# Six PSUM banks in one pool, products of heads and of a layer's last group issued elsewhere, and a first load in halves: a two-layer trunk on one core

## The chip, the core and the metric

The kernel runs on one core of a Trainium2 chip. The metric is the device time of one execution in microseconds, from runs on the chip. Five engines of the core work at the same time, each through its own instructions in order: TensorE (PE, with its weight loads apart as PEld), VectorE (DVE), ScalarE (ACT), GpSimd (POOL) and SyncE (SP, which here only issues transfers). PE writes its results to PSUM, eight banks of 128 partitions x 512 fp32 values; DVE and ACT read them from there into SBUF.

## The reference

Two layers over x of 512 tokens x 1024 features in fp32 (batch 1). Cut to what is computed:

```python
for i in range(2):
    xn = rmsnorm(x, norm1_g[i])
    u_pool, q, k, v, g_a, g_b = split(xn @ w_in[i])       # 1024 wide each
    # 4 heads, two q/k maps of 128 each, v of 256
    q = rotary(rmsnorm(q, q_norm_g[i])); k = rotary(rmsnorm(k, k_norm_g[i]))
    p = softmax(mask(q @ k.T * 128 ** -0.5))              # chunk-causal, chunks of 64
    o = (p[map 0] - lam * p[map 1]) @ v
    o = rmsnorm(o, subln_g[i]) * (1 - lam_init)
    pool = concat over 4 groups of (mean of the last 2/4/8/16 tokens of u - u) @ w_pool
    merged = sigmoid(g_a) * pool * pool_scale + sigmoid(g_b) * o
    x = x + merged @ w_out[i]
    gate, up = split(rmsnorm(x, norm2_g[i]) @ w_ffn_in[i])   # 2816 wide each
    x = x + (silu(gate) * up) @ w_ffn_out[i]
```

## The kernel before

**Products.** Every fp32 operand is split into a high part `...h`/`hi` (a cast on ACT) and a remainder `...l`/`lo` (a subtraction on DVE), in `split` (L208; the function's rows have L210). A product of two operands is three matmuls: high x high, high x low, low x high (`product`, L294; `in_turn`/`three`, L277 to L292). A product of 128 tokens x 512 columns over the 1024 features is 24 matmuls. Weights come in pieces of 512 KB in the order of `weight_plan`, into seven `raw` buffers, and are split into `whi`/`wlo` (six buffers). Almost all of a layer's DVE work beside the splits is reading results from PSUM.

**Order.** A scheduler of the framework sets the order on each engine from the order in which the code issues the work; buffers and banks are handed out in turn by pool name, and an instruction that takes a buffer waits for its last reader. Work that has to wait for a transfer or another engine is put off by hand: `later(delay, f)` puts `f` on a heap with a due time in PE columns, and `run_due` runs what is due between two products. PSUM has four pools: `mm` (three banks), `sc` (two), `tr` (two), and one bank `oy`, whose two halves take the attention outputs in turn (`o_ps`) and which as a whole takes every second out-unit of the feed-forward part (`unit_bank`).

**A layer, first half.** The four heads in the order 3, 2, 1, 0 (`ORDER`). `attention(j)` makes q and k of the head in four token tiles `t`; `evicted` reads each bank (squares on ACT, `r` on POOL at L344, `qn` on DVE at L597), rotates, and transposes by way of a transfer to HBM and back (`turned`). Then follow, by due times, `turn` (splits into `qh`, `ql`), `scores(t)` (bank `sc`, softmax into `pr`), `turn_prob` (splits into `ah`, `al`) and `weighted(t)` (the product with v; `mt` at L565 reads the result). Between two heads `mix(i)` calls `merged`: the pooled inputs u (`up`, `us`, then `uh`, `ul`), the two gate products (`ta`, L686), the pool's product with `pw`, and the merged result of the head as `mh`/`ml` (L214, L215). `project_out` (L762) multiplies the merged result of the first or second head with its rows of w_out and adds it to the residual `res`; `attention` calls it through `then` in the third and fourth head, after tile 0. `last_out` (L771) does the same for the last two heads together, eight outputs with 12 matmuls each: six of head 1, six of head 0.

**Second half.** `odd_group`, then five groups of four hidden blocks. Each group makes its gate and up products with seven instead of eight smaller products (`PRODUCTS`, in the order 1, 4, 5, 6, 2, 7, 3), from sums of inputs and weights; pairs of banks are `a` (`sc`), `b` (`mm`) and `c` (`tr`). Product 5 writes `c`, DVE reads it into `cah`/`cal` (L928) after product 7, and product 3 writes `c` anew. `UNITS` says after which product of which group an out-unit stands (24 matmuls with the hidden values of an earlier group). Last come the out-units of the last two groups.

**The start.** Twelve bf16 matmuls on zeros run first. `first_step(i)` loads two feature blocks of weights (`wr`) and of x (`xr`), 512 KB each; for i = 0 the split and the scaling by the gain (`xh`, `xl`) are already done in halves.

## Time and profile before

| | before |
|---|---|
| median of 3 runs | 1393.08 us (1391.87 to 1394.55) |
| the profiled execution | 1394.02 us, its span 1392.2 us |
| granted TensorE clock | 1.00 |
| PE busy | 1375.2 us (99%), 6242 matmuls |
| DVE busy | 1045.5 us (75%), 1979 instructions |
| ACT busy | 703.3 us (51%) |
| POOL busy | 117.7 us (8%) |
| HBM traffic | 160 GB/s over the span |

The rows of the trace name an engine, the line of the kernel, the output tile `<-` the input tiles, a shape and a count. In brackets stands the idle time of the engine just before, and what ended it. The table of waits adds these idle times by line and releaser: total, times, longest. In the chain of waits each piece starts where the one before released it.

### The profile page before, as it was taken

To read this page: it belongs to the slowest core of one execution; us is meant where nothing else is said; L and a number is where in the kernel's file an instruction comes from. 1 tells how busy PE (TensorE), PEld (TensorE's weight loads), DVE (VectorE), ACT (ScalarE), POOL (GpSimd) and SP (SyncE) were. 2 spreads that over 40 slices of the span, in tenths; PEclk is the share of its full clock that TensorE was granted. 3 is DMA by queue.
4 is the path that set the end of the run, shared out by engine and by line. 5 is a ranking of instruction groups with operands and counts; after the bars stand their busy time and mean duration, and the time that the engine had idled before them with its cause. 6 is when DMAs were issued, how large, how long until landed. Compare 5 with 4: busy or idle time off the path is not lost.

```text
span 1392.2 us, 18593 instructions
## 1 busy us (share of the span) xinstructions
PE 1375.2 (99%) x6242; PEld 1138.3 (82%) x6242; DVE 1045.5 (75%) x1979; ACT 703.3 (51%) x1321; POOL 117.7 (8%) x139
## 2 busy tenths in 40 slices
PE   9999999999999999999999999999999999999998
PEld 7888788887888888887887787888878888888877
DVE  7769788686968768677668896877868687676782
ACT  7445353454756545554345543434447565565540
POOL 1010100000101001000010101000001010000000
PEclk9999999999999999999999999999999999999999
DMA  7333454445667868676434445544446788677741
GB/s 300 113 124 112 143 164 128 146 130 146 133 178 197 224 190 230 161 199 195 134 102 138 124 142 179 161 133 126 150 137 136 188 211 212 195 207 179 183 137 61
DMA packets 140783, 224.52 MB, mean 161 GB/s; under 512 B 40848, under 2 KB 88464, under 8 KB 140688
## 3 DMA queue, kind: packets, MB, share of 16 engines
q1 hardware_dynamic: 130176, 187.65, 42.0%
q0 software_dynamic: 9216, 33.56, 13.9%
q10 hardware_dynamic: 1296, 2.12, 0.5%
q8 instruction: 49, 0.80, 0.2%
q14 instruction: 46, 0.38, 0.1%
HBM read 194.04 MB, written 29.23 MB: 160 GB/s over the span
## 4 chain that ended last, share of the span: by engine, by line
PE 89%; DVE 6%; issue 1%; POOL 1%; DMA 1%; ACT 1%; SPq 0%; DVEq 0%; POOLq 0%; ACTq 0%
PE mm L299 11%; PE mm L300 11%; PE mm L301 11%; PE mm L281 8%; PE mm L282 8%; PE mm L280 8%; PE tr L280 3%; PE tr L281 3%; PE tr L282 3%; PE oy L281 3%; PE oy L280 3%; PE oy L282 3%; PE sc L280 3%; PE sc L281 3%; PE sc L282 3%
## 5 line engine op out<-in xcount | busy, mean ns | idle before, releaser
L210 ACT CAST whi<-raw 128x1024 fp32r<-128x1024 f32 (+1 forms) x221 | 230.2, 1047 | 175.7 <-PE mm L300 42.0
L210 DVE TENSOR_TENSOR wlo<-raw,whi 128x1024 fp32r<-128x1024 f32 (+1 forms) x221 | 267.0, 1212 | 63.1 <-ACT whi L210 62.2
L299 PE MATMUL mm<-whi,xh 128*128 128x512 f32 x480 | 188.9, 394 | 1.0 <-DVE qn L597 1.0
L301 PE MATMUL mm<-whi,xl 128*128 128x512 f32 x480 | 187.3, 390 | 0.0
L300 PE MATMUL mm<-wlo,xh 128*128 128x512 f32 x480 | 187.3, 390 | 0.0
L301 PEld LDWEIGHTS mm<-whi,xl 128*128 128x128 f32 x480 | 90.2, 188 | 19.0
L299 PEld LDWEIGHTS mm<-whi,xh 128*128 128x128 f32 x480 | 90.3, 188 | 18.6 <-PE mm L301 1.4
L300 PEld LDWEIGHTS mm<-wlo,xh 128*128 128x128 f32 x480 | 90.3, 188 | 17.3
L236 POOL DMA_DIRECT2D wlo<-in_wts x64 | 56.1, 877 | 552.3 <-ACT wlo L235 423.0
L344 POOL TENSOR_TENSOR r<-r,mhalf 128x1 f32<-128x1 f32 (+1 forms) x64 | 56.7, 887 | 525.0 <-DVE r L343 422.0
L300 PE MATMUL mm<-xl,whi 128*128 128x512 f32 x256 | 99.9, 390 | 0.0
L299 PE MATMUL mm<-xh,whi 128*128 128x512 f32 x256 | 99.9, 390 | 0.0
L301 PE MATMUL mm<-xh,wlo 128*128 128x512 f32 x256 | 99.7, 390 | 0.0
L703 DVE TENSOR_TENSOR res<-mm,res 128x512 f32<-128x512 f32 x96 | 65.3, 682 | 32.3 <-PE mm L282 27.5
L235 ACT ACTIVATE wlo<-raw 128x1024 fp32r<-128x1024 f32 x64 | 67.7, 1057 | 26.8 <-PE mm L281 25.2
L234 ACT CAST whi<-raw 128x1024 fp32r<-128x1024 f32 x64 | 66.6, 1040 | 18.3 <-issue 17.7
L280 PE MATMUL oy<-fh,whi 128*128 128x512 f32 (+1 forms) x180 | 69.7, 387 | 0.0
L281 PE MATMUL oy<-fl,whi 128*128 128x512 f32 (+1 forms) x180 | 69.7, 387 | 0.0
L282 PE MATMUL oy<-fh,wlo 128*128 128x512 f32 (+1 forms) x180 | 69.7, 387 | 0.0
L280 PE MATMUL mm<-fh,whi 128*128 128x512 f32 (+1 forms) x176 | 68.1, 387 | 0.0
L282 PE MATMUL mm<-fh,wlo 128*128 128x512 f32 (+1 forms) x176 | 68.1, 387 | 0.0
L281 PE MATMUL mm<-fl,whi 128*128 128x512 f32 (+1 forms) x176 | 68.1, 387 | 0.0
(244 smaller groups left out, 3231.4 us busy)
## 6 DMA issues: line engine op xcount, KB each, us to landing
raw<-in_wts SPq DMA_DIRECT2D x244, 512.0 KB, 4.1
wlo<-in_wts POOLq DMA_DIRECT2D x64, 512.0 KB, 6.2
away<-near SPq DMA_DIRECT2D x72, 256.0 KB, 2.3
near<-away SPq DMA_DIRECT2D x288, 64.0 KB, 2.2
away<-near SPq DMA_DIRECT2D x28, 128.0 KB, 1.7
near<-away SPq DMA_DIRECT2D x112, 32.0 KB, 2.4
res<-in_x_t SPq DMA_DIRECT2D x4, 512.0 KB, 7.7
pwr<-in_pool_w ACTq DMA_DIRECT2D x8, 256.0 KB, 2.6
```

Of the source, the lines that this page charges most:

```text
L210: return nc.scalar.copy(hi, src), nc.vector.tensor_sub(lo, src, hi.bitcast(F32))
L234: nc.scalar.copy(hi, raw)
L235: made[0] = nc.scalar.activation(lo, raw, AF.Copy, scale=-1.0)
L236: nc.gpsimd.dma_start(lo.rearrange("p a b -> p (a b)"), wts[piece_no], accum_op=ALU.add)
L280: nc.tensor.matmul(acc, lhsT=ah, rhs=bh, start=start, stop=False, **check)
L281: nc.tensor.matmul(acc, lhsT=ah, rhs=bl, start=False, stop=False, **check)
L282: last = nc.tensor.matmul(acc, lhsT=al, rhs=bh, start=False, stop=stop, **check)
L299: nc.tensor.matmul(acc, lhsT=ah, rhs=bh, start=i == 0, stop=False)
L300: nc.tensor.matmul(acc, lhsT=ah, rhs=bl, start=False, stop=False)
L301: last = nc.tensor.matmul(acc, lhsT=al, rhs=bh, start=False, stop=i == n - 1)
L344: nc.gpsimd.tensor_tensor(r, r, mhalf[:, :width], op=ALU.pow)
L703: return nc.vector.tensor_add(res[d][:, cs], acc, res[d][:, cs])
```

## The change

It has five parts. The pools `tr` and `oy` are gone and `mm` has six banks; transposes, attention outputs and out-units draw from it. `project_out` is called after tile 1. `last_out` issues, for its first pair of outputs, the products of head 1 into both banks and then those of head 0. The out-unit (2, 3) of the last group stands after product 7 instead of after product 4; the weight plan follows. The first weights and the first x are loaded in two transfers each, in turn.

```diff
-         (3, 7): [(2, 0)], (3, 3): [(2, 1)], (4, 1): [(2, 2)], (4, 4): [(2, 3)]}
+         (3, 7): [(2, 0)], (3, 3): [(2, 1)], (4, 1): [(2, 2)], (4, 7): [(2, 3)]}
...
     def mm_ps():
-        return ps.tile([P, 512], F32, name="mm", tag="mm", bufs=3)
+        return ps.tile([P, 512], F32, name="mm", tag="mm", bufs=6)
...
-    def tr_ps():
-        return ps.tile([P, 512], F32, name="tr", tag="tr", bufs=2)
-
-    oy = ps.tile([P, 2, VD], F32, name="oy", tag="oy")
-    turns = [0]
-
-    def o_ps():
-        turns[0] += 1
-        return oy[:, turns[0] % 2, :]
+    tr_ps = mm_ps
...
-    def in_turn(acc, pairs, start=True):
+    def in_turn(acc, pairs, start=True, stop=True):
...
-                last = three(acc, a, b, start and not i, i == len(pairs) - 1)
+                last = three(acc, a, b, start and not i, stop and i == len(pairs) - 1)
...
-        nc.sync.dma_start(wr, wts[i].rearrange("p (a s) -> p a s", a=2))
-        nc.sync.dma_start(xr, x_t[i].rearrange("p (a s) -> p a s", a=2))
+        for ks in (slice(0, 1), slice(1, 2)) if not i else (slice(0, 2),):
+            for to, src in ((wr, wts), (xr, x_t)):
+                nc.sync.dma_start(to[:, ks, :], src[i].rearrange("p (a s) -> p a s", a=2)[:, ks, :])
...
-                o = s_ps()[:, :VD] if at_start and t % 2 else o_ps()
+                o = mm_ps()[:, :VD]
...
-                if not t and then is not None:
+                if t == 1 and then is not None:
                     then()
...
-        def unit_bank(n):
-            return oy.rearrange("p a b -> p (a b)") if n % 2 else mm_ps()
...
         def last_out(x):
             for i in range(4):
                 w = piece(4)
+                accs = [mm_ps() for _ in range(2)]
+                pairs = [[(cols(w, a)[2 * n + h], (ms[j][0][:, h, :], ms[j][1][:, h, :]))
+                          for n, j in enumerate(ORDER[2:]) for h in range(2)] for a in range(2)]
+                if not i:
+                    for a in range(2):
+                        in_turn(accs[a], pairs[a][:2], stop=False)
                 for a in range(2):
-                    acc = mm_ps()
-                    in_turn(acc, [(cols(w, a)[2 * n + h], (ms[j][0][:, h, :], ms[j][1][:, h, :]))
-                                  for n, j in enumerate(ORDER[2:]) for h in range(2)])
-                    x.added = add_out(i + 4 * a, acc)
+                    in_turn(accs[a], pairs[a][0 if i else 2:], i > 0)
+                    x.added = add_out(i + 4 * a, accs[a])
                 x.put(i)
...
-                units[0] += 1
-                acc = unit_bank(units[0])
+                acc = mm_ps()
```

The numbers of matmuls and of the other instructions stay as they are, but for the two more transfers on SP. The lines of the changed kernel are eight to ten lower for the same code (L299 becomes L290).

In the last group of layer 1 PE goes from product 7 (`xr` operands, the `mm` bank) straight to product 3 (`xh`, the `tr` bank of `cah`):

```order
L280 MATMUL mm_12340<-whi_12422,xrh_10125 128x512
L281 MATMUL mm_12340<-wlo_12423,xrh_10125 128x512
L282 MATMUL mm_12340<-whi_12422,xrl_10126 128x512
L280 MATMUL tr_12121<-whi_12485,xh_9886 128x512
L281 MATMUL tr_12121<-wlo_12486,xh_9886 128x512
L282 MATMUL tr_12121<-whi_12485,xl_9887 128x512
L280 MATMUL tr_12121<-whi_12485,xh_9886 128x512
L281 MATMUL tr_12121<-wlo_12486,xh_9886 128x512
```

In the changed kernel the unit's 24 matmuls (`fh`, `fl`, two banks of 12) stand between them:

```order
L271 MATMUL mm_12377<-whi_12459,xrh_10180 128x512
L272 MATMUL mm_12377<-wlo_12460,xrh_10180 128x512
L273 MATMUL mm_12377<-whi_12459,xrl_10181 128x512
L271 MATMUL mm_12527<-fh_11196,whi_12523 128x512
L272 MATMUL mm_12527<-fl_11197,whi_12523 128x512
...
L272 MATMUL mm_12541<-fl_11199,whi_12523 128x512
L273 MATMUL mm_12541<-fh_11198,wlo_12524 128x512
L271 MATMUL mm_12190<-whi_12566,xh_9941 128x512
L272 MATMUL mm_12190<-wlo_12567,xh_9941 128x512
L273 MATMUL mm_12190<-whi_12566,xl_9942 128x512
```

What moved is the unit, from behind product 4 of the same group to the place between the two.

In layer 1, second head, PE issues the weighted product of tile 2 (`ah`, `al`, into `oy`) behind both gate products (`mm_7854` is the second) and the first matmul with `pw`:

```order
L299 MATMUL mm_7854<-xh_6352,whi_7615 128x512
L300 MATMUL mm_7854<-xl_6353,whi_7615 128x512
L301 MATMUL mm_7854<-xh_6352,wlo_7616 128x512
L299 MATMUL mm_7883<-uh_7624,pw_7621 128x512
L299 MATMUL oy_66<-vh_7356,ah_7731 128x256
L300 MATMUL oy_66<-vl_7357,ah_7731 128x256
L300 MATMUL mm_7883<-ul_7625,pw_7621 128x512
L301 MATMUL mm_7883<-uh_7624,pw_7621 128x512
L299 MATMUL mm_7922<-uh_7624,pw_7621 128x512
L301 MATMUL oy_66<-vh_7356,al_7732 128x256
L299 MATMUL oy_66<-vh_7356,ah_7731 128x256
```

In the changed kernel it stands (into `mm_7862`) behind the first gate product, `mm_7841`, and ahead of the second, `mm_7900`:

```order
L290 MATMUL mm_7841<-xh_6388,whi_7658 128x512
L291 MATMUL mm_7841<-xl_6389,whi_7658 128x512
L292 MATMUL mm_7841<-xh_6388,wlo_7659 128x512
L290 MATMUL mm_7862<-vh_7399,ah_7775 128x256
L291 MATMUL mm_7862<-vl_7400,ah_7775 128x256
L292 MATMUL mm_7862<-vh_7399,al_7776 128x256
...
L291 MATMUL mm_7862<-vl_7400,ah_7775 128x256
L292 MATMUL mm_7862<-vh_7399,al_7776 128x256
L290 MATMUL mm_7900<-xh_6388,whi_7640 128x512
L291 MATMUL mm_7900<-xl_6389,whi_7640 128x512
```

It moved up by the 24 matmuls of a gate product and one of the pool's. On DVE the split that makes its `al` stood here, behind the sums `us` of the pooled inputs and one weight split:

```order
L686 TENSOR_TENSOR ta_7851<-mm_7796,hg_6484 128x512
L661 MEMSET us_7787 128x16
L662 TENSOR_TENSOR us_7787<-us_7784 128x512
L210 TENSOR_TENSOR wlo_7952<-raw_7949,whi_7951 128x1024
L665 TENSOR_TENSOR head_7790<-us_7787,tab_69 128x16
L666 SCALAR_TENSOR_TENSOR us_7787<-us_7787,up_7775 128x496
L210 TENSOR_TENSOR al_7732<-pr_7526,ah_7731 128x384
L668 TENSOR_TENSOR us_7787<-head_7790,up_7775 128x16
L686 TENSOR_TENSOR ta_7880<-mm_7854,hg_6484 128x512
```

In the changed kernel it stands behind the same sums, without that weight split, and ahead of the evacuation `ta` of the second gate as before:

```order
L678 TENSOR_TENSOR ta_7897<-mm_7841,hg_6523 128x512
L653 MEMSET us_7832 128x16
L654 TENSOR_TENSOR us_7832<-us_7829 128x512
L648 MEMSET up_8666 128x16
L657 TENSOR_TENSOR head_7835<-us_7832,tab_68 128x16
L658 SCALAR_TENSOR_TENSOR us_7832<-us_7832,up_7820 128x496
L660 TENSOR_TENSOR us_7832<-head_7835,up_7820 128x16
L653 MEMSET us_8669 128x16
L201 TENSOR_TENSOR al_7776<-pr_7569,ah_7775 128x384
```

On DVE it moved by one weight split only.

## The prediction

> **What bounds the kernel now.** I read the page's busy times first, then the waits of TensorE, then the rows around each wait.

> ```profile
> span 1392.2 us, 18593 instructions
> PE 1375.2 (99%) x6242; PEld 1138.3 (82%) x6242; DVE 1045.5 (75%) x1979; ACT 703.3 (51%) x1321; POOL 117.7 (8%) x139
> ```

> TensorE is the bound: 6242 matmuls fill 99% of the span. The change keeps every matmul, so it can only win idle time of PE. All of that idle time stands in one short table (total, times, longest):

> ```profile
> PE mm L299 <- DVE qn L597: 3.5, 2, 2.4
> PE tr L280 <- DVE cah L928: 3.1, 2, 1.6
> PE oy L299 <- DVE mt L565: 1.7, 3, 0.8
> PE mm L391 <- DVE us L661: 1.2, 1, 1.2
> PE mm L280 <- ACT mh L214: 1.2, 2, 0.6
> PE tr L462 <- DVE xh L454: 0.8, 1, 0.8
> PE mm L299 <- ACT mh L214: 0.6, 1, 0.6
> PE mm L281 <- DVE ml L215: 0.5, 2, 0.2
> PE sc L300 <- DVE ql L210: 0.4, 1, 0.4
> PE sc L301 <- DVE al L210: 0.3, 1, 0.3
> PE mm L300 <- DVE ml L215: 0.2, 1, 0.2
> ```

> The L391 row is the wait of the warm-up matmuls for a memset and stays, as does the `al` row (first head of layer 0). The rest sums to 12.0 us. The table counts from the modelled end of the matmul before, so it is short. These rows (start, duration) give the correction:

> ```profile
> 646.06 0.39 PE L280 MATMUL mm<-whi,xrh 128*128 128x512 f32 x1
> 646.29 0.39 PE L281 MATMUL mm<-wlo,xrh 128*128 128x512 f32 x1
> 646.51 0.39 PE L282 MATMUL mm<-whi,xrl 128*128 128x512 f32 x1
> 648.47 0.47 PE L280 MATMUL tr<-whi,xh 128*128 128x512 f32 x1 [1.57 <-DVE cah L928]
> ```

> A matmul lasts 0.39 us but the next starts 0.227 us after it, so each wait costs some 0.16 us more than the table says: here 648.47 - 646.51 - 0.227 = 1.73, against 1.57. With 0.16 for each of these 15 waits, some 14 us are there to win: a perfect change ends near 1380, 1% below the 1394.0 us of the profiled execution (span 1392.2 and 1.8 around it). That execution is 0.9 above the median 1393.08; I sum against 1394.0 and take 0.9 off at the end. A difference under 0.2% (2.8 us) is about what a measurement cannot tell from none.

> **The change part by part.**

> *Halves at the start.* The chain of waits at the start, and the DMA rows for sizes:

> ```profile
> 0.74 4.61 DMA raw<-in_wts
> 5.38 0.63 ACT whi L210
> 6.03 0.60 DVE wlo L210
> 6.67 0.50 DVE xh L454
> 7.31 0.47 PE tr L462
> 1.19 5.30 PE L391 MATMUL mm<-cold 128*128 128x512 bf16 x12 [1.19 <-DVE us L661]
> raw<-in_wts SPq DMA_DIRECT2D x244, 512.0 KB, 4.1
> pwr<-in_pool_w ACTq DMA_DIRECT2D x8, 256.0 KB, 2.6
> ```

> The cast, the subtraction and the scaling already work on halves; only the two transfers (weights, x) are whole. 256 KB land in 2.6 us elsewhere, 512 KB in 4.1: 1.5 less. The chain behind it keeps its length, and the warm-up matmuls end at 1.19 + 5.30 = 6.49 by the record (the last of them could be followed at about 6.3), so at most 1.0 can be won. At worst nothing is: the two more issues on SP push the later transfers back. I take 0.8, near the cap, because 1.5 is well over it.

> [...]

> *`project_out` after the second token tile.* It was called after tile 0 and consumed `mh`/`ml` of an earlier head too early. In layer 0:

> ```profile
> 146.45 0.40 PE L301 MATMUL mm<-mh,wlo 128*128 128x512 f32 x1
> ...
> 148.50 0.39 PE L301 MATMUL mm<-mh,wlo 128*128 128x512 f32 x1
> ```

> Three steps take 2.05 instead of 0.68: 1.37 lost. One more tile is 24 matmuls, 24 x 0.227 = 5.4 us, in front of it: gone (between 1.37 and 0, and the cover is four times the need).

> *`last_out`, both layers.* The two head-2 products of both accumulators now come first, 12 matmuls instead of 6 ahead of the first use of the last head.

> ```profile
> 340.83 0.39 PE L280 MATMUL mm<-mh,whi 128*128 128x512 f32 x1
> ...
> 343.62 0.39 PE L282 MATMUL mm<-mh,wlo 128*128 128x512 f32 x1
> ```

> Five steps took 2.79 instead of 1.13: 1.66. The cover is 6 x 0.227 = 1.36; I take 1.3 in each layer, 2.6 (bounds 0 and 3.3). The first `put` comes 1.4 later for it; it feeds the odd group, behind three more rounds of 12 matmuls.

> *The unit after product 7.* In the last group of each layer product 3 waits for `cah` (1.73 above, about the same in layer 1). Now 24 matmuls, 5.4 us, stand between: both go, 3.4. Product 5 loses the unit that stood ahead of it. Groups 0 and 1 have none there either, and no wait of such a product is in the table: nothing.

> *Six banks, heads of layer 1.* Gone: the longer of the two waits for `qn`, 2.4 + 0.16 = 2.6 (a `project_out` whose bank `qn` still reads), and the other, 1.1 + 0.16 = 1.2 (a bank too); the three of `oy` behind `mt`, 1.7 + 3 x 0.16 = 2.2, since the weighted products no longer share one bank; the 0.6 at `ql`. That is 6.6.

> But the same pool lets the order issue the weighted products of the first two heads earlier, ahead of where their operands are ready. The second head, before (DVE rows, PE row, then windows with busy time of PE, PEld, DVE, ACT, POOL):

> ```profile
> 806.19 0.69 DVE L657 TENSOR_TENSOR up<-mm,hg 128x512 f32<-128x512 f32 x1 [2.05 <-PE mm L301]
> ...
> 823.21 1.22 DVE L210 TENSOR_TENSOR wlo<-raw,whi 128x1024 fp32r<-128x1024 f32 x1
> ...
> 825.02 0.56 DVE L210 TENSOR_TENSOR al<-pr,ah 128x384 fp32r<-128x384 f32 x1
> 825.01 0.39 PE L299 MATMUL oy<-vh,ah 128*128 128x256 f32 x1
> 826.05 0.28 PE L301 MATMUL oy<-vh,al 128*128 128x256 f32 x1
> 810.00:815.00 5.00, 5.00 (x25) 4.18 (x24) 4.95 (x15) 0.20 (x1) 0.54 (x1) 1.00 0.38 120
> 815.00:820.00 5.00, 5.00 (x26) 4.22 (x25) 4.51 (x15) 2.12 (x7) 0.98 (x1) 1.00 0.50 169
> 820.00:825.00 5.00, 5.00 (x23) 3.95 (x21) 5.00 (x12) 4.03 (x6) 0.00 (x0) 1.00 0.66 216
> ```

> The product of tile 2 uses `al` 0.5 us after DVE wrote it. The order now puts it one gate product ahead: 24 matmuls and one of the pool's, 25 x 0.227 = 5.7 us earlier, so PE asks for `al` at about 819.7 on this clock (its first matmul, 825.01 - 5.7 = 819.3, and two more). On DVE only the 1.22 of `wlo` goes from in front of `al`. From `up` at 806.19, where DVE last waited for PE, `al` ended after 825.58 - 806.19 = 19.4 us; less 1.22, and less the 0.54 us that DVE is idle in the three windows, 17.6. PE needs it after 819.7 - 806.2 = 13.5. New wait: 4.1, with ends 0 (DVE less behind than counted) and 6.3 (`al` as late as before). Behind this product in PE's queue stand the second gate's, and then everything: nothing hides it.

> The first head, tile 3:

> ```profile
> 773.50 1.22 DVE L210 TENSOR_TENSOR wlo<-raw,whi 128x1024 fp32r<-128x1024 f32 x1
> ...
> 775.35 0.48 DVE L565 SCALAR_TENSOR_TENSOR mt<-oy,r,hg 128x256 f32<-128x256 f32 x1 [0.43 <-POOL r L344]
> 775.75 0.68 DVE L210 TENSOR_TENSOR al<-pr,ah 128x512 fp32r<-128x512 f32 x1
> 776.51 0.35 PE L301 MATMUL oy<-vh,al 128*128 128x256 f32 x1
> ```

> `al` comes behind two `wlo`, and now ahead of that `mt`: it would end 1.1 to 1.8 earlier, about 775. PE asks 2.2 (the `oy` waits gone) and about 2.0 (its new place) earlier, near 772.3. New wait between 0 and 776.43 - 772.3 = 4.1; I take 3.0. The scores of tile 2 of the next head stand 1.3 us earlier on PE, behind the same `ql` split that cost 0.6: 0 to 2.1, taken as 1.7. Together +8.8 against -6.6: the front of layer 1 costs 2.2 us net, with ends -6.6 (no new wait) and +5.9.

> *The other banks.* A bank of the pool now comes round after six uses instead of three, and nearly all uses are of 24 matmuls, so there are two products more between a read and the next write. `cah`'s two banks stay held from product 5 to 3, leaving four for pairs: nothing.

> Sum: -0.8 - 1.4 - 2.6 - 3.4 + 2.2 = -6.0, so 1388.0 for an execution like the profiled one, and 1387.1 against the median.

> **The rivals.**
> 1. *All waits go and no new one comes.* The weighted products find their splits ready. For it: DVE is 75% busy over the span, and only one `al` wait (0.3) exists today. Against it: the three windows above, DVE 14.46 of 15 us. Then -8.2 - 6.6 = -14.8: 1379.2 on the profiled clock, 1378.3 against the median. Half of it (A or B alone appears) gives 1382 to 1383.
> 2. *The new waits eat the gain.* The front of layer 1 at its upper ends, the start wins nothing: -7.4 + 5.9 = -1.5, some 1391.6: no change that a measurement can tell.
> 3. *Slower: every head pays.* What is computed above for two heads, a weighted product issued ahead of its split on DVE, happens in the others too. Each costs 3 to 4 us. With the mean of the two, 3.6, two more such waits use up the gain (-6.0 + 7.2), three make the kernel measurably slower (-6.0 + 10.8 = +4.8), and six end at 1394.0 - 6.0 + 21.6 - 0.9 = 1408.7. Against it: in the remaining heads the order shifts these products and their splits by about the same amount, and the waits table has no `al` wait there to start from.
> 4. *The moved units do not help:* `cah` waits for DVE's `wlo` queue, so product 3 could wait all the same if DVE were more than 5.4 us behind. It was 1.73 behind. Worth at most 3.4: 1390.5.

> **How the numbers follow.** Forecast (the front of layer 1 loses a few us, the rest wins): 0.50, 1383 to 1390. Rival 1, under 1383: 0.24. Rivals 2 and 4, 1390 to 1396: 0.18. Rival 3, over 1396: 0.08. The likeliest is the first, 1387.1. The first and second together reach down to 1378.3 and the third's likelier half up to 1392: the range 1378.5 to 1392 leaves out some 2 in 10. Cases under 1390.3 are faster by over 0.2%: 0.50 + 0.24 less a little at the edge, 0.72; no change 0.19; slower 0.09.

> **What would show it.** In the new profile the rows `cah L928`, `qn L597` and `oy <- mt` are missing from PE's waits, and `mh`/`ml` are down to under 0.5 in total. PE's first product starts at 6.4 to 6.7 instead of 7.31. New rows `<- DVE al L210` stand near 772 and 815, of 3 and 4 us, and one `<- DVE ql` near 790. If these are missing, rival 1 holds and DVE was less behind than I counted; if they stand in layer 0 or in the later heads too, rival 3. The busy time of PE stays near 1375. It would be wrong most of all if DVE's own order lets `al` pass the `us` sums, which my count of its rows takes as fixed.

## The result, and the profile after

The changed kernel takes 1391.68 us (median of 21 runs, 1390.02 to 1392.82) against 1393.62 us for the kernel before (21 runs): ratio 0.9985, 95% interval 0.9978 to 0.9992. It is faster by some 2 us, a third of the 6 us that were forecast, and inside what the prediction called no change. The profiled executions differ by as much: spans of 1389.7 and 1392.2 us.

The waits of PE after the change (us in total, times, longest):

```profile
PE mm L290 <- ACT ah L201: 6.4, 2, 3.2
PE mm L382 <- DVE us L653: 1.2, 1, 1.2
PE sc L290 <- ACT pr L520: 0.9, 1, 0.9
PE mm L297 <- DVE qn L367: 0.6, 1, 0.6
PE sc L291 <- DVE ql L201: 0.5, 1, 0.5
PE mm L292 <- DVE up L648: 0.4, 1, 0.4
PE mm L292 <- DVE al L201: 0.3, 1, 0.3
```

Of the waits that the change was to remove only the one for `ql` is left (0.5, was 0.4); `cah`, `mt`, `mh`/`ml`, and `qn` as the reader of a bank are gone from the list. Half of their sum is back as two waits for `ah`, in the first and second head of layer 1, at the two places that the prediction named. But these two explain only part of it. Around the first (start, duration of PE's matmuls):

```profile
765.97 0.39 PE L292 MATMUL mm<-whi,xl 128*128 128x512 f32 x1
769.60 0.39 PE L290 MATMUL mm<-vh,ah 128*128 128x256 f32 x1 [3.24 <-ACT ah L201]
...
773.18 0.63 PE L290 MATMUL mm<-whi,xh 128*128 128x512 f32 x1
773.60 0.60 PE L291 MATMUL mm<-wlo,xh 128*128 128x512 f32 x1
774.03 0.40 PE L292 MATMUL mm<-whi,xl 128*128 128x512 f32 x1
```

From 773.18 to 774.03 a matmul of 512 columns takes 0.42 us from start to start instead of 0.227. The windows show why (busy time of PE, PEld, DVE, ACT, POOL, then the granted clock, the share of DMA and GB/s). The borders here are those at which the granted clock changes:

```profile
767.21:770.63 3.42, 1.03 (x5) 0.72 (x5) 3.42 (x9) 2.85 (x4) 0.82 (x1) 1.00 0.44 120
770.63:774.04 3.41, 3.35 (x14) 2.97 (x14) 3.38 (x5) 0.00 (x0) 0.00 (x0) 0.50 0.15 48
818.42:821.83 3.41, 0.82 (x4) 0.61 (x5) 3.22 (x12) 1.65 (x3) 0.00 (x0) 1.00 0.79 258
821.83:825.24 3.41, 3.41 (x13) 2.92 (x12) 1.41 (x5) 0.47 (x2) 0.54 (x1) 0.50 0.52 128
```

Behind each wait TensorE gets half its clock for 3.41 us, which by estimate costs half of that, 1.7 us, each time. The profiled execution of the kernel before has no such stretch: its mean granted clock is 1.000.

To see where the rest went I added up, for each stretch of the two traces, what the steps from one PE start to the next take beyond the median step of the same two widths in the kernel before (us; the changed kernel's stretches are shifted by less than 5 us):

| stretch | what stands there | forecast | before | after | change |
|---|---|---|---|---|---|
| 0 to 20 | first weights and x | -0.8 | 3.5 | 2.3 | -1.2 |
| 20 to 60 | transposes of the first head | 0 | 0.9 | 1.7 | +0.8 |
| 60 to 200 | `project_out`, layer 0 | -1.4 | 3.4 | 1.7 | -1.7 |
| 200 to 500 and 900 to 1200 | `last_out` | -2.6 | 3.4 | 0.5 | -2.9 |
| 500 to 690 and 1200 on | product 7, unit, product 3 | -3.4 | 3.1 | -0.6 | -3.7 |
| 690 to 750 | layer 1, `qn` and its bank | -1.2 | 1.4 | 1.2 | -0.2 |
| 750 to 785 | weighted products, first head | +0.8 | 2.7 | 5.6 | +2.9 |
| 785 to 800 | scores behind `ql` | +1.1 | 0.7 | 0.8 | +0.1 |
| 800 to 835 | weighted product, second head | +4.1 | 0.2 | 6.2 | +6.0 |
| 835 to 900 | `project_out`, layer 1 | -2.6 | 2.8 | 0.1 | -2.7 |
| sum | | -6.0 | 22.1 | 19.5 | -2.6 |

Two gains came back at once as another wait. At the start PE begins at 5.93 instead of 7.31, but the transposes wait for `qn`, which is no earlier:

```profile
28.70 0.39 PE L456 MATMUL sc<-whi,xl 128*128 128x512 f32 x1
29.72 0.63 PE L297 MATMUL mm<-ident,qn 128*128 128x128 f32 x4 [0.63 <-DVE qn L367]
```

And where the bank read by `qn` had held PE for 1.2 at 731, the scores now wait 0.9; their chain goes back through an exp (`pr`), a table load of ACT (the 1.28 at L520; the timeline calls it ACT_TABLE_LOAD) and a cast to a transfer (chain of waits, start and length):

```profile
726.60 3.04 DMA near<-away
...
729.96 0.61 ACT qh L201
...
730.59 1.28 ACT L520
...
731.88 0.47 ACT pr L520 x2
732.35 0.04 issue
732.39 0.39 PE sc L290
```

### The profile page after: what moved, and what is told of

It reads as the page before. It is cut to its first block, busy times and chain, and to the rows that moved or that the text cites. A ratio compares the mean times of both kernels' runs of the same rounds, so it can differ in the third digit from the quotient of the medians.

```text
span 1389.7 us, 18568 instructions
## 1 busy us (share of the span) xinstructions
PE 1375.8 (99%) x6242; PEld 1142.0 (82%) x6242; DVE 1042.5 (75%) x1979; ACT 704.1 (51%) x1321; POOL 118.2 (9%) x139
## 3 DMA queue, kind: packets, MB, share of 16 engines
q10 hardware_dynamic: 1296, 2.12, 0.5%
## 4 chain that ended last, share of the span: by engine, by line
PE 93%; DVE 3%; issue 1%; DMA 1%; POOL 1%; ACT 0%; SPq 0%; DVEq 0%; POOLq 0%; ACTq 0%
PE mm L272 14%; PE mm L273 14%; PE mm L271 14%; PE mm L292 13%; PE mm L290 13%; PE mm L291 13%; PE sc L271 3%; PE sc L273 3%; PE sc L272 3%; PE sc L291 1%; PE sc L292 1%; PE sc L290 1%; DVE qn L589 1%; POOL r L335 1%; DVE wlo L201 1%
## 5 line engine op out<-in xcount | busy, mean ns | idle before, releaser
L290 PE MATMUL mm<-whi,xh 128*128 128x512 f32 x480 | 189.0, 394 | 0.0
L291 PE MATMUL mm<-wlo,xh 128*128 128x512 f32 x480 | 187.5, 391 | 0.0
L292 PE MATMUL mm<-whi,xl 128*128 128x512 f32 x480 | 187.3, 390 | 0.0
L273 PE MATMUL mm<-fh,wlo 128*128 128x512 f32 (+1 forms) x356 | 137.8, 387 | 0.0
L272 PE MATMUL mm<-fl,whi 128*128 128x512 f32 (+1 forms) x356 | 137.8, 387 | 0.0
L271 PE MATMUL mm<-fh,whi 128*128 128x512 f32 (+1 forms) x356 | 137.8, 387 | 0.0
L692 DVE TENSOR_TENSOR res<-mm,res 128x512 f32<-128x512 f32 (+1 forms) x145 | 98.1, 680 | 43.1 <-PE mm L273 41.8
L290 PEld LDWEIGHTS mm<-whi,xh 128*128 128x128 f32 x480 | 90.4, 188 | 17.4
L290 PE MATMUL mm<-xh,whi 128*128 128x512 f32 x256 | 100.3, 392 | 0.0
L273 PE MATMUL mm<-whi,xl 128*128 128x512 f32 x224 | 87.2, 389 | 0.0
L271 PE MATMUL mm<-whi,xh 128*128 128x512 f32 x224 | 87.2, 389 | 0.0
L272 PE MATMUL mm<-wlo,xh 128*128 128x512 f32 x224 | 87.2, 389 | 0.0
L271 PEld LDWEIGHTS mm<-fh,whi 128*128 128x128 f32 x356 | 66.9, 188 | 13.6
## 6 DMA issues: line engine op xcount, KB each, us to landing
raw<-in_wts SPq DMA_DIRECT2D x243, 512.0 KB, 3.9
wlo<-in_wts POOLq DMA_DIRECT2D x64, 512.0 KB, 6.1
away<-near SPq DMA_DIRECT2D x72, 256.0 KB, 2.4
pwr<-in_pool_w ACTq DMA_DIRECT2D x8, 256.0 KB, 2.7
away<-pr SPq DMA_DIRECT2D x7, 256.0 KB, 2.0
```

The lines of the kernel that those rows point to most:

```text
L271: nc.tensor.matmul(acc, lhsT=ah, rhs=bh, start=start, stop=False, **check)
L272: nc.tensor.matmul(acc, lhsT=ah, rhs=bl, start=False, stop=False, **check)
L273: last = nc.tensor.matmul(acc, lhsT=al, rhs=bh, start=False, stop=stop, **check)
L290: nc.tensor.matmul(acc, lhsT=ah, rhs=bh, start=i == 0, stop=False)
L291: nc.tensor.matmul(acc, lhsT=ah, rhs=bl, start=False, stop=False)
L292: last = nc.tensor.matmul(acc, lhsT=al, rhs=bh, start=False, stop=i == n - 1)
```

## The experiments

Theory 1: the four other parts win what was forecast. The pool takes it back, because the weighted products that draw from it are ordered ahead of `ah` and `al` at two places, and the clock falls behind each wait. The rivals: the removed waits come back elsewhere whatever the pool, the size of the pool is at fault, or the slow matmuls come from something other than the idle time.

**1. The old pools.** The change without its second part:

```diff
-        return ps.tile([P, 512], F32, name="mm", tag="mm", bufs=6)
+        return ps.tile([P, 512], F32, name="mm", tag="mm", bufs=3)
...
-    tr_ps = mm_ps
+    def tr_ps():
+        return ps.tile([P, 512], F32, name="tr", tag="tr", bufs=2)
+
+    oy = ps.tile([P, 2, VD], F32, name="oy", tag="oy")
...
-                o = mm_ps()[:, :VD]
+                o = s_ps()[:, :VD] if at_start and t % 2 else o_ps()
...
-                acc = mm_ps()
+                acc = unit_bank(units[0])
```

> The changed kernel with the four PSUM pools of before; the other four parts stay. Theory 1 (the pool's order costs two waits of 3.4 and 3.9 us for ah/al in layer 1 and a slow TensorE clock behind each, the other parts win what was forecast): start 0.6 (1.4 less a new wait of 0.8 for the transposes), project_out 1.4, last_out 2.7, the unit 3.5, and the wait at 838 perhaps: 8 to 11 us faster than before, ratio 0.992 to 0.994. Rival (the other parts' waits come back elsewhere, because VectorE and ScalarE are no earlier): within 3 us of before, ratio over 0.998.

1384.3 us, ratio 0.9939 (0.9926 to 0.9951): 8 us faster. The order of the weighted products on PE in layer 1's first two heads is that of before, and the mean granted clock is 1.000 in every run. The waits of `oy` are still there, and one for `qn`:

```profile
PE oy L299 <- DVE mt L566: 1.5, 3, 0.8
...
PE mm L299 <- DVE qn L598: 1.0, 1, 1.0
```

The other parts won what was forecast, and the wait of `project_out` in layer 1 went too (2.8 to 1.3 in the stretch 835 to 900): moving it behind tile 1 does that without six banks, but a wait of the scores (0.7, or 0.9 from start to start) took part of its place.

**2. The pool alone.** The kernel before with `mm` of six banks for `mm`, `tr` and `oy`:

```diff
-        return ps.tile([P, 512], F32, name="mm", tag="mm", bufs=3)
+        return ps.tile([P, 512], F32, name="mm", tag="mm", bufs=6)
...
+    tr_ps = mm_ps
...
-                o = s_ps()[:, :VD] if at_start and t % 2 else o_ps()
+                o = mm_ps()[:, :VD]
...
-                acc = unit_bank(units[0])
+                acc = mm_ps()
```

> The kernel before with the one pool of six banks alone. Theory 1: the same two waits with idle times over 3 us and matmuls at half speed behind them; 4 to 7 us slower than before, ratio 1.003 to 1.005. Rival (the pool is not where the gain goes): ratio 0.998 to 1.000.

1399.19 us, ratio 1.0043 (1.0029 to 1.0056). Slower by 6 us, as theory 1 had it; by the ratios the pool costs as much on top of the other parts (0.9985 against 0.9939). Here the clock stays low for two windows after the first wait:

```profile
769.08:772.49 3.41, 1.18 (x6) 0.64 (x4) 3.41 (x12) 2.83 (x5) 1.39 (x1) 1.00 0.46 131
772.49:775.90 3.41, 2.37 (x8) 2.08 (x9) 3.41 (x7) 1.51 (x3) 0.00 (x0) 0.50 0.40 112
775.90:779.32 3.42, 3.42 (x14) 3.03 (x14) 2.44 (x3) 0.91 (x7) 0.00 (x0) 0.50 0.01 6
```

The wait reached into the second window, PE was not busy all through it, and the clock came back only after the third.

**3. The wait filled with matmuls.**

```diff
+                late = 1536 if layer and j == ORDER[0] and t == 3 else 0
...
+                first = layer and j == ORDER[0] and t == 3
+                for _ in range(24 if first else 0):
+                    nc.tensor.matmul(o, lhsT=xh[:, 0, token(0)], rhs=xh[:, 0, :VD], start=True, stop=True)
```

> The changed kernel with 24 matmuls of 256 columns ahead of the weighted product of tile 3 of the first head of layer 1, which compute nothing that is used; they take 2.7 us of the 3.4 us in which PE waits there. Theory 1 (a clock that falls after the idle time): PEclk stays 1.00 in 770 to 775, the matmuls behind keep 0.23 us from start to start, and the kernel is 1 to 2 us faster than the changed one although it does more. Rival (the slow matmuls come from what else runs in that stretch): 0.66 in that window as before, and no gain or a loss.

1385.89 us, ratio 0.995 (0.9938 to 0.9963). The clock stays at 1.00, and so does the pace behind the wait:

```profile
766.71 3.03 PE L555 MATMUL mm<-xh 128*128 128x256 f32 x24
770.15 0.39 PE L290 MATMUL mm<-vh,ah 128*128 128x256 f32 x1 [0.41 <-ACT ah L201]
771.42 0.39 PE L292 MATMUL mm<-vh,al 128*128 128x256 f32 x1 [0.77 <-DVE al L201]
767.98:771.40 3.42, 2.26 (x17) 1.85 (x15) 3.42 (x10) 2.64 (x4) 0.60 (x1) 1.00 0.41 108
771.40:774.81 3.41, 3.39 (x20) 3.01 (x21) 3.38 (x4) 0.00 (x0) 0.00 (x0) 1.00 0.16 50
```

The slow pace came from the clock and the clock from the idle time: VectorE and ScalarE do the same work in that stretch. The first line of the edit also puts the product off by 1536 columns, three matmuls. The gain is larger than expected: 5.4 us between the spans of the two traces (1389.7 and 1384.3), and most of it is not from this wait. By the stretches of the table above the first head wins 3.6 us, of which the 24 matmuls take back 2.9 (0.12 each); the scores behind `ql` win 0.8, and the second head 4.4 (1.8 lost there instead of 6.2). In the second head the edit also shifted the scheduler's order: `al` stands ahead of `ta` on DVE and no longer behind it, and the clock stayed at 1.00 there too.

**4. Both waits moved away.** The cast `ah` of the first head issued ahead of four weight casts on ACT, and the weighted product of the second head put off by one gate product:

```diff
+                raws = [loaded()[0] for _ in range(KD // 2)]
+                with tc.issue_after(cast[0].ins):
+                    w = [p for raw in raws for p in rows_of(parts(raw))]
...
-                later(AV_WAIT if at_start else AV_AWAY, lambda: weighted(t, ah, al))
+                late = 12288 if layer and j == ORDER[1] and t == 2 else 0
+                later(AV_WAIT if at_start else AV_AWAY + late, lambda: weighted(t, ah, al))
```

> The changed kernel with both waits taken away: the cast ah of tile 3 of the first head of layer 1 is issued ahead of the four weight casts of the next v product, and the weighted product of tile 2 of the second head is put off by one gate product. Theory 1: both waits under 1.5 us, no slow stretch, 8 to 11 us faster than the changed kernel, some 1382, ratio to before 0.991 to 0.994. Rival (VectorE is behind in any order, so the wait comes up again at the next product): less than 4 us faster than the changed kernel.

1391.51 us, ratio 0.9991 (0.9982 to 1.0). No faster than the changed kernel, so the rival was right: the waits only moved. In the first head `ah` was ready 2.5 us sooner than in the changed kernel and `al` 1.8 us, which was still 1.5 us too late:

```profile
767.08 0.39 PE L290 MATMUL mm<-vh,ah 128*128 128x256 f32 x1 [0.66 <-ACT ah L201]
769.06 0.54 PE L292 MATMUL mm<-vh,al 128*128 128x256 f32 x1 [1.47 <-DVE al L201]
765.72:769.13 3.41, 1.27 (x7) 0.60 (x5) 2.97 (x12) 3.20 (x6) 0.59 (x1) 1.00 0.43 121
769.13:772.55 3.42, 3.42 (x13) 3.18 (x14) 3.42 (x4) 3.42 (x5) 0.00 (x0) 0.50 0.45 123
```

Neither of these waits is as long as 1.7 us, and the clock fell all the same. In the second head the wait of tile 2 was gone, but tile 3, next in the queue and not put off, waited instead, and the clock was low for two windows.

**5. One pool of five, the bank `oy` kept.** As experiment 1, but the transposes draw from `mm` (the lines against experiment 1):

```diff
-        return ps.tile([P, 512], F32, name="mm", tag="mm", bufs=3)
+        return ps.tile([P, 512], F32, name="mm", tag="mm", bufs=5)
...
+    tr_ps = mm_ps
```

> The changed kernel with one pool of five banks (mm and tr together) and the bank oy kept for the attention outputs and every second out-unit. Here the order of the weighted products on PE is that of before. Theory 1 (what costs is that the weighted products draw from the pool): none of the two long waits, no slow stretch, the wait for qn near 727 shorter or gone, the three waits of oy (2.0) there: 1382 to 1385, ratio 0.992 to 0.9945. Rival (five or six banks in one pool cost it, whatever draws from it): ratio over 0.997.

1383.92 us, ratio 0.9933 (0.9921 to 0.9946). Sharing banks with the transposes costs nothing against the 1384.3 of experiment 1. It brings little either: the wait for `qn` is gone, and a second one of the scores for `pr` has come.

**6. `tr` kept apart, the weighted products in `mm`.** The opposite cut of the changed kernel:

```diff
-        return ps.tile([P, 512], F32, name="mm", tag="mm", bufs=6)
+        return ps.tile([P, 512], F32, name="mm", tag="mm", bufs=4)
...
-    tr_ps = mm_ps
+    def tr_ps():
+        return ps.tile([P, 512], F32, name="tr", tag="tr", bufs=2)
```

> The changed kernel with the pool tr kept apart (two banks), mm with four banks, oy gone: the weighted products and the out-units draw from mm. Theory 1: both long waits near 766 and 817, half clock behind them, time within 2 us of the changed kernel, ratio 0.997 to 1.0. Rival (the size of the pool decides): no such waits, near 1384.

1393.08 us, ratio 0.9998 (0.9989 to 1.0007), with both waits:

```profile
PE mm L292 <- ACT ah L203: 6.4, 2, 3.2
770.00:775.00 5.00, 4.87 (x20) 4.12 (x21) 4.85 (x6) 0.59 (x2) 0.00 (x0) 0.66 0.19 52
```

The order on PE in these heads is that of the changed kernel. So the size of the pool is not the cause; what matters is whether the weighted products draw from it. How the scheduler comes to the order no run shows. A reading that fits is that with `oy` they get their one bank late, and with a share in `mm` they come as soon as the scheduler believes their operands to be there.

**7. Fewer unused matmuls.** Eight instead of 24 (the lines against experiment 3):

```diff
-                for _ in range(24 if first else 0):
+                for _ in range(8 if first else 0):
```

> As the kernel with 24 unused matmuls ahead of the weighted product of tile 3, but with 8 of them (0.9 us), and three matmuls of the next product between: an idle time of 2 to 2.6 us is left. Theory 1 (the clock falls only behind more than some 3 us of idle time, since the wait of 2.4 in the kernel before left it at 1.00): PEclk 1.00 in 770 to 775. Rival (any wait of a few us lowers it in proportion): about 0.75 there.

1391.4 us in its one run. Both theories missed: in the first head, with no wait over 1.5 us, the clock went to one half, not to 0.75 and not to 1.00:

```profile
769.95 0.39 PE L290 MATMUL mm<-vh,ah 128*128 128x256 f32 x1 [1.37 <-ACT ah L201]
771.23 0.56 PE L292 MATMUL mm<-vh,al 128*128 128x256 f32 x1 [0.31 <-DVE al L201]
767.87:771.28 3.41, 1.73 (x9) 0.81 (x7) 3.41 (x10) 2.55 (x4) 0.51 (x1) 1.00 0.44 119
771.28:774.69 3.41, 3.41 (x13) 3.22 (x14) 3.38 (x4) 0.00 (x0) 0.00 (x0) 0.50 0.19 57
```

In the kernel before, the single wait of 2.43 at 838 left it at full speed. The two windows on the same grid there (the grid counted on from 7.20, where its clock first rose):

```profile
836.63:840.05 3.42, 1.89 (x9) 1.24 (x7) 2.04 (x8) 1.01 (x7) 1.59 (x2) 1.00 0.88 299
840.05:843.46 3.41, 2.51 (x11) 2.11 (x12) 3.41 (x12) 0.00 (x0) 0.00 (x0) 1.00 0.40 119
```

The long wait of before was cut in two by a border of the grid. So in these traces the length of a single wait does not decide, but how much PE does within one window of the grid. The busy time of the profile is not an exact measure of it. Of the windows at full clock that were read here, those with 1.84 us or more kept it (1.84 from 645.49 in the kernel before, the least in its trace until PE's work ends; 1.89 above; 2.26 in experiment 3) and those with 1.27 or less lost it (1.27 and 0.97 in experiment 4, 1.18 in experiment 2, 1.03 and 0.82 in the changed kernel); between the two, this run has a window in the second head that kept it with 1.55, where the one above lost it with 1.73:

```profile
815.65:819.07 3.42, 1.55 (x7) 0.94 (x5) 3.39 (x11) 0.76 (x2) 0.00 (x0) 1.00 0.42 153
819.07:822.48 3.41, 1.63 (x10) 1.42 (x11) 2.72 (x9) 0.89 (x2) 0.00 (x0) 1.00 0.82 242
```

The second of these, with 1.63, lost it. A matmul's record is longer than the step to the next one (0.39 us against 0.227 for 512 columns, 0.28 against 0.12 for 256, the latter from 771.64 to 772.72 in experiment 3). What tells the windows between 1.27 and 1.84 apart was not shown.

**8. The halves alone**, in the kernel before:

```diff
-        nc.sync.dma_start(wr, wts[i].rearrange("p (a s) -> p a s", a=2))
-        nc.sync.dma_start(xr, x_t[i].rearrange("p (a s) -> p a s", a=2))
+        for ks in (slice(0, 1), slice(1, 2)) if not i else (slice(0, 2),):
+            for to, src in ((wr, wts), (xr, x_t)):
+                nc.sync.dma_start(to[:, ks, :], src[i].rearrange("p (a s) -> p a s", a=2)[:, ks, :])
```

> The kernel before with the first weights and x in two transfers each, nothing else. Theory 1: the first product starts near 5.9 instead of 7.3, and 0.8 of it is given back where the transposes of the first head wait for qn near 29; 0.5 to 0.7 us faster, ratio 0.9995, not to be told from none by the time. Rival (the start's gain is kept): no wait near 29, 1.3 us faster.

1393.64 us, ratio 1.0003 (0.9993 to 1.0012): no difference by the time. The trace shows the first product at 5.93 and the wait of the transposes, as in the changed kernel:

```profile
29.78 0.63 PE L306 MATMUL tr<-ident,qn 128*128 128x128 f32 x4 [0.63 <-DVE qn L376]
```

**9. Two banks for the heads.** Four `mm` (with `tr`), two `sc`, and two whole banks `oy` for attention outputs and out-units (one call of `token_stats` draws from `sc` instead of `mm`):

```diff
-        return ps.tile([P, 512], F32, name="mm", tag="mm", bufs=6)
+        return ps.tile([P, 512], F32, name="mm", tag="mm", bufs=4)
...
+    def o_ps():
+        return ps.tile([P, 512], F32, name="oy", tag="oy", bufs=2)
...
-                o = mm_ps()[:, :VD]
+                o = o_ps()[:, :VD]
...
-                acc = mm_ps()
+                acc = o_ps()
```

> The changed kernel with the eight banks as four mm (tr among them), two sc and two whole banks oy for the attention outputs and all out-units. Here PE has the weighted product of tile 3 eight matmuls (1.8 us) later than in the changed kernel and that of tile 2 of the second head 21 matmuls (4.8 us) later. Theory 1 (the places of these two decide): a wait of at most 1.5 us at the first, none at the second, clock 1.00, the three waits of 1.7 in all for a shared oy bank gone: 1381 to 1384, ratio 0.991 to 0.994. Rival (a pool in which the weighted products take banks in turn brings the long waits): near 1390.

1382.68 us, ratio 0.992 (0.9906 to 0.9934): faster than both kernels, as theory 1 had it. It is the lowest median of all, but its interval overlaps that of experiment 5. Its longest wait behind the start is 0.9 us:

```profile
PE sc L293 <- ACT pr L523: 0.9, 1, 0.9
...
PE oy L295 <- DVE al L204: 0.6, 2, 0.3
PE oy L293 <- ACT ah L204: 0.6, 1, 0.6
```

## Why the prediction was wrong

It was wrong in its sum: 6.0 us of gain against 2.6 in the traces and 1.9 in the medians. The direction and the places were right.

- **The failed step is the price of the new waits** ("Together +8.8 against -6.6: the front of layer 1 costs 2.2 us net"). It priced a wait by the time in which PE stands still. The waits themselves came close: 3.4 at the first head (forecast 3.0) and 3.3 + 0.6 at the second (4.1). But each left so little work in a window (1.03 and 0.82 us of 3.41) that the window behind it ran at half the clock: 2 x 1.7 = 3.4 us by estimate. The two stretches together cost 8.9 where 4.9 was forecast. That 3.4 is also the whole gap between 6.0 and 2.6 is luck: the other misses below nearly cancel. The prediction's own rows did not show this price: in the profiled execution of the kernel before, no wait had left a window with under 1.84 us of busy PE, and the clock stayed at 1.00. The windows that lost the clock were not idle either: PE was busy for 0.82 and 1.03 us in those of the changed kernel and for up to 1.73 in experiment 7. The prediction did not weigh a loss of clock.
- **The 1.2 at 731 did not go away.** The bank was free, but the scores behind it then waited for the exp, which stands behind a transfer, a cast and a table load of 1.28 us (-0.2 for -1.2). Experiments 1 and 5 show the same exchange: with three banks in `mm` the wait for `qn` (1.0) and none of the scores there, with five the reverse (0.9).
- **The start:** 1.2 won where 0.8 was forecast, and 0.8 given back at the transposes, which the prediction did not name. PE began 1.38 earlier, right behind the warm-up matmuls, so the cap of 1.0 was too low.
- **`ql`** was overpriced: 0.1 instead of 1.1. This (1.0) and the larger gains of the unit, `project_out` and `last_out` (8.3 against 7.4) hid 1.9 us of the errors above.
- **The releaser was half right:** at both places `ah`, the cast on ACT, ended the long wait, not `al` on DVE. In the first head it stands behind three weight casts. In the second it stands behind a tanh (L679) that had itself waited for DVE's `ta`, so there DVE was behind, as forecast, one step further back:

```profile
766.10 2.92 ACT L201 CAST whi<-raw 128x1024 fp32r<-128x1024 f32 x3
768.93 0.62 ACT L201 CAST ah<-pr 128x512 fp32r<-128x512 f32 x1
819.53 0.63 ACT L679 ACTIVATE ta<-ta 128x512 f32<-128x512 f32 x1 [5.74 <-DVE ta L678]
820.06 0.50 ACT L201 CAST ah<-pr 128x384 fp32r<-128x384 f32 x1
```

Experiment 4 shows that an earlier `ah` is not enough in the first head: `al` is late as well.

- **Rival 1** (no new waits) is what experiments 1, 5 and 9 come to, by keeping the weighted products out of the shared pool, though none reaches its 1378.3. **Rival 2** (the new waits eat the gain, some 1391.6) has the measured time, and its front of layer 1 (+5.9) is close to that of the table (+6.1). It has it by luck: it took longer waits at full clock, while the runs had waits near the forecast's length and the half clock behind them. **Rival 3** (every head pays) did not happen: the two places are the only waits for `ah`. **Rival 4** (the moved unit does not help) did not happen either: it won 3.7.

Not settled: why the edit of experiment 3 shifted the order in the second head; the shares of `project_out`, `last_out` and the unit, which are read from stretches, as none of the three ran alone; and how much of the clock's loss falls on a given run. The clock first rises at 7.20 us in the trace of before and at 6.04 in that of the changed kernel, and the grid is counted from there, so one and the same wait may be cut by a border in one run and not in the next. The runs on record fit that. In the changed kernel the mean granted clock goes from 0.996 (four runs, 1392.39 to 1392.48 us) to 0.999 (its fastest, 1390.02), while it is 1.000 in all runs of experiments 1, 3, 5 and 9. The kernel before has both: beside experiment 1, seven runs at 0.999 took 1393.25 to 1394.86 us and eight at 1.000 took 1391.43 to 1392.56. But its profiled execution took 1394.02 at 1.000, so its spread is not the clock's alone.

## What to carry to other kernels

A pool that frees an instruction from a buffer also frees the scheduler to put it earlier, ahead of the operands it needs; look at where it now stands against the instructions that feed it, on each of their queues. Look, beside the length of a wait of TensorE, at how much PE does in the window around it: here the clock stayed at 1.00 behind windows with 1.84 us or more of 3.41 and fell to 0.50 behind those with 1.27 or less, and each window at half clock cost some 1.7 us more by estimate. And before a wait is counted as won, ask which of the next instruction's other inputs was late too.
